# An encoder trunk on eight cores: the 31-tap depthwise convolution as a four-phase block convolution instead of diagonal matmuls

## Chip, cores and metric

The kernel runs on one Trainium2 chip, on all 8 cores, each with its own quarter of one sequence (two dies of four cores). The metric is the device time of the slowest core in microseconds. Some executions fall into a slower state: the cores of one die (of both in one of the runs) show a lower granted TensorE clock, 0.81 to 0.97 instead of 0.98, and the program takes 1 to 17% longer. In the fast runs all eight cores show 0.96 to 0.99, mostly 0.98.

In some runs that still count as fast, two cores of one die sit at a clock of 0.96 to 0.97 and finish 10 to 20 us late. Where that happened it is said, and "clean" means a fast run in which no core did so. "Slow clock": behind a wait the profile shows a granted clock of 0.50, in before for 3.4 to 10.5 us and once, at the gap between the halves, for 34 us. Eight matmuls then take up to 3.57 us instead of 1.89 (before, at 1028.45 us). The first projection's eight take 3.57 us too, but there the record still shows 1.00.

## The reference, cut to what matters

Two layers; every layer is a token mixer, a cross-attention into 256 memory tokens and a SwiGLU block, each behind an RMSNorm and with a residual add. Only the mixer of layer 0 is rebuilt by the change.

```python
D_A = D_B = 512; A_KERNEL = 31; B_KERNEL = 3        # D_MODEL = 1024, SEQ = 8192

def conv_pair_mixer(n, w_in, a_conv_w, a_conv_b, a_ln_g, a_ln_b, b_conv_w, b_conv_b, w_out):
    z = n @ w_in                                        # (B, S, 2560)
    a_val, a_gate, b_h, b_gb, b_gc = jnp.split(z, [...], axis=-1)
    # A: GLU -> depthwise conv (31, centred) -> LayerNorm over channels -> swish
    a = a_val * jax.nn.sigmoid(a_gate)
    a = depthwise_conv(a, a_conv_w, a_conv_b)
    a = jax.nn.silu(layer_norm(a, a_ln_g, a_ln_b))
    # B: B * conv3(C * h)
    b = b_gb * depthwise_conv(b_gc * b_h, b_conv_w, b_conv_b)
    return jnp.concatenate([a, b], axis=-1) @ w_out
```

## The kernel before

Each core has 2048 tokens and works through them in two halves of 1024; a half is two tiles of 512 tokens. Channels lie on the partitions, tokens along the free dimension. The program is a list of operations per engine; a "slot" object records who wrote and who read a buffer, and the semaphore waits follow from it. A small queue of deferred operations (`push`, `tick`) drops the RMSNorm squares and scalings between matmul groups. Weights stream through `NS = 4` slots of SBUF, all issued from GpSimd.

The A convolution multiplies each of four blocks of 128 channels by 31 diagonal matrices and accumulates over the taps in PSUM. Of the 128 rows that feed one output row of such a matmul only one carries anything but zeros. The order of the mixer is: A projection, A convolution with its LayerNorm, B projection, B convolution with its gate, output projection.

```python
    def setup_diag(self, js, with_b, after=()):          # built by GpSimd at the start
        for j in js:
            for k0 in range(0, 31, 4):
                ...
                P.op("pool", "tensor_tensor", [self.ident_s, self.vec_s] + list(after), [self.diagA_s[j]],
                     out=self.diagA[:, j, k0:k0 + nk, :], in0=<identity>, in1=<taps>, op=ALU.mult)
        ...                                              # diagB likewise, 3 taps

    def l0_mixer(self):
        tiles = [(tt, TT) for tt in range(NTT)] + [(-1, H2)]     # two tiles of 512, then the halo of 2x16 tokens
        ...
        for tt, n in tiles:
            for j in range(4):
                bv = self.linear(...)                    # value and gate projections
                bg = self.linear(...)
                ...                                      # a_ext[:, j, ...] = value * sigmoid(gate)
        self.flush(keep="setup")
        for tt in range(NTT):
            for j in range(4):
                b = self.bank()
                pairs = [(self.diagA[:, j, k, :], self.a_ext[:, j, tt * TT + k + 1:tt * TT + k + 1 + TT])
                         for k in range(31)]
                self.mm_group(b, pairs, TT, reads=[self.a_ext_s[j], self.diagA_s[j]])
                cb.append(b)
            ...                                          # ac = conv + bias; acb = ac; sqa = ac**2
            self.mm_group(b1, [(self.ones[:, :], self.acb[:, j, :]) for j in range(4)], TT, ...)   # sums over
            self.mm_group(b2, [(self.ones[:, :], self.sqa[:, j, :]) for j in range(4)], TT, ...)   # the channels
            ...                                          # mean, rstd; y[:, j] = silu((ac - mean) * rstd * g + b)
        ...                                              # B: project h and C, multiply into a_ext
        for tt in range(NTT):
            for j in range(4):
                pairs = [(self.diagB[:, j, k, :], self.a_ext[:, j, tt * TT + k:tt * TT + k + TT]) for k in range(3)]
                self.mm_group(bcv, pairs, TT, reads=[self.a_ext_s[j], self.diagB_s])
                bgb = self.linear(...)
                ...                                      # y[:, 4 + j] = (conv + bias) * gate
        self.proj_residual("ev_out", 0, self.y, self.y_s, KC, nxt=V_GXA)
```

Between the halves the final norm goes through a separate buffer `nf`, is stored, and then x of the next half is loaded and normalised:

```python
            for tt in range(NTT):
                self.store_tile(h, tt, jobs[tt])
                if h + 1 < NHALF:
                    self.load_tile(h + 1, tt)
                    if tt == 0:
                        self.load_halo(h + 1)
```

The softmax here doesn't subtract the row's maximum and nothing guards it: scores larger than these inputs give would overflow.

## Time and profile before

| | us |
|---|---|
| median of 16 runs | 1992.5 |
| fast runs | 1990.7 to 1995.7 |
| the two slow runs among them | 2325.8, 2335.3 |

The first fence is from the page of the profile. The numbered lines give busy time (share of the span) and instructions of each engine; a line of the groups reads: source line, engine, operation, output<-inputs, shape, count | busy us, mean ns | idle time of the engine just before.

```profile
span 1989.4 us, 24567 instructions; the slowest of 8 cores (1970.3 to 1989.4 us)
...
PE 1845.9 (93%) x8826; PEld 839.5 (42%) x8826; DVE 619.6 (31%) x968; ACT 576.7 (29%) x961; POOL 118.1 (6%) x194
...
PE 84%; DVE 4%; ACT 4%; DMA 4%; issue 3%; DVEq 0%; SPq 0%; ACTq 0%; POOLq 0%
...
L401 PE MATMUL ps<-a_ext,diagA 128*128 128x512 bf16 x496 | 109.9, 383 | 0.0
```

TensorE (PE) is busy 93% of the span, and the chain of work that ended last (the third line shown) is 84% TensorE. So time is to be had only from fewer matmul columns or from TensorE's 143.5 us of idle time. The diagonal convolution is 496 matmuls of 512 columns and 109.9 us.

The list of what TensorE waited for; the columns are total us, times, and the longest wait:

```profile
PE ps L72 <- ACT sq L72: 54.0, 22, 13.1
PE ps L401 <- DVE nT L72: 27.3, 4, 12.8
...
PE ps L401 <- DMA wbuf<-w_xq: 10.4, 4, 3.5
PE ps L401 <- DVE a_ext L72: 8.3, 2, 7.7
```

The timeline of TensorE, from several windows; the columns are start, duration (us), engine, line, operation, output<-inputs, shape, count, and in brackets the idle time before it with what released it:

```profile
38.60 3.57 PE L401 MATMUL ps<-nT,wbuf 128*128 128x512 bf16 x8 [12.79 <-DVE nT L72]
...
83.82 1.02 PE L401 MATMUL ps<-nTh,wbuf 128*128 128x32 bf16 x32 [7.67 <-DVE a_ext L72]
84.67 28.97 PE L401 MATMUL ps<-a_ext,diagA 128*128 128x512 bf16 x124
...
117.10 26.98 PE L401 MATMUL ps<-a_ext,diagA 128*128 128x512 bf16 x124
...
148.75 14.69 PE L401 MATMUL ps<-nT,wbuf 128*128 128x512 bf16 x64
...
197.69 5.34 PE L401 MATMUL ps<-y,wbuf 128*128 128x512 bf16 x24
...
231.29 1.04 PE L401 MATMUL ps<-memnT,wbuf 128*128 128x256 bf16 x8
...
1028.45 3.57 PE L401 MATMUL ps<-nT,wbuf 128*128 128x512 bf16 x8 [7.20 <-DVE nT L72]
```

These lines are milestones. The first projection starts at 38.6 us. The A convolution with its sums runs from 84.7 to 148.75 us. The output projection begins at 197.69, and at 231.29 the keys of the memory tokens follow. The second half's first projection starts at 1028.45 us, 31.7 us after the first half's last matmul of the down projection.

VectorE (same columns): at the start the eight scalings of x tile 0, 1.36 us each, and later one product.

```profile
27.55 10.90 DVE L72 SCALAR_TENSOR_TENSOR nT<-hT,vec,rs 128x512 bf16<-128x512 f32 x8 [27.55 <-ACT rs L72]
...
157.94 0.69 DVE L72 TENSOR_TENSOR ac<-ac,rs 128x512 f32<-128x512 f32 x1
```

### The profile page before, as it was taken

Reading aid. Unit: us, or ns where it says so; the run is one execution under the profiler, and the core shown is the slowest. Engines: PE = TensorE matmul, PEld = TensorE weight load, DVE = VectorE, ACT = ScalarE, POOL = GpSimd, SP = SyncE. Lnnn points to the kernel's source line nnn. Section 1 sums busy time; section 2 is a strip of 40 time slices with the busy share of each in tenths; the row PEclk is TensorE's granted clock in tenths of the full one; section 3 lists DMA queues with packets and bytes.
Section 4 is the critical chain, followed back from the end, with each engine's and each line's share of the span. In section 5 each row is a group of like instructions: output and inputs, shape, how many; then the busy total and the mean of one; then the engine's idle time right before and its main releaser. Section 6 shows DMA issues by size and latency. Waiting matters only on the chain.

```text
span 1989.4 us, 24567 instructions; the slowest of 8 cores (1970.3 to 1989.4 us)
## 1 busy us (share of the span) xinstructions
PE 1845.9 (93%) x8826; PEld 839.5 (42%) x8826; DVE 619.6 (31%) x968; ACT 576.7 (29%) x961; POOL 118.1 (6%) x194
## 2 busy tenths in 40 slices
PE   3899899999989899999949999999999999999996
PEld 0344444444434444444414444444444444444443
DVE  2423415121156324121132423342111661532113
ACT  2323353111133353111142423531111433521111
POOL 8000000000000000000000000000000000000000
PEclk9899999999999999999969999999999999999998
DMA  7204662433434632334352067233345327234252
GB/s 169 43 1 74 99 104 43 74 68 69 81 59 86 112 58 49 79 64 88 61 182 44 1 106 127 43 54 74 64 88 93 64 51 143 41 64 85 51 88 85
DMA packets 28949, 150.60 MB, mean 76 GB/s; under 512 B 2976, under 2 KB 3360, under 8 KB 17440
## 3 DMA queue, kind: packets, MB, share of 16 engines
q0 software_dynamic: 21456, 130.30, 37.0%
q1 hardware_dynamic: 7376, 18.74, 3.0%
q8 instruction: 74, 1.21, 0.2%
q14 instruction: 43, 0.35, 0.1%
HBM read 270.92 MB, written 8.39 MB: 140 GB/s over the span
## 4 chain that ended last, share of the span: by engine, by line
PE 84%; DVE 4%; ACT 4%; DMA 4%; issue 3%; DVEq 0%; SPq 0%; ACTq 0%; POOLq 0%
PE ps L401 82%; DMA wbuf<-w_xq 2%; PE ps L72 2%; DVE nT L72 2%; DMA hT<-x_in 2%; ACT t L72 1%; ACT L72 1%; DVE nf L72 1%; ACT pT L72 1%; ACT sq L72 1%; ACT rs L72 1%; DVE hT L72 0%; PE ps L723 0%; DVE v_ln L72 0%; DVE memnT L72 0%
## 5 line engine op out<-in xcount | busy, mean ns | idle before, releaser
L401 PE MATMUL ps<-nT,wbuf 128*128 128x512 bf16 x4224 | 935.9, 382 | 30.4 <-DVE nT L72 20.0
L401 PEld LDWEIGHTS ps<-nT,wbuf 128*128 128x128 bf16 x4224 | 413.5, 98 | 528.4 <-issue 48.2
L72 ACT ACTIVATE t<-ps 128x512 f32<-128x512 f32 (+1 forms) x288 | 164.2, 574 | 566.2 <-PE ps L401 539.1
L401 PE MATMUL ps<-hid,wbuf 128*128 128x512 bf16 x1408 | 313.7, 379 | 0.0
L72 ACT ACTIVATE sq<-hT 128x512 bf16<-128x512 f32 x224 | 137.9, 627 | 484.5 <-DVE hT L72 439.4
L72 DVE TENSOR_TENSOR hid<-ps,t 128x512 bf16<-128x512 f32 x176 | 121.0, 691 | 468.9 <-PE ps L401 468.9
L72 DVE TENSOR_TENSOR hT<-hT,ps 128x512 f32<-128x512 f32 x192 | 130.8, 687 | 384.1 <-PE ps L401 384.1
L401 PEld LDWEIGHTS ps<-hid,wbuf 128*128 128x128 bf16 x1408 | 137.7, 98 | 165.8
L72 DVE SCALAR_TENSOR_TENSOR nT<-hT,vec,rs 128x512 bf16<-128x512 f32 x192 | 135.7, 774 | 90.6 <-ACT rs L72 90.6
L72 PE MATMUL ps<-sq,ones 128*128 128x512 bf16 (+2 forms) x248 | 89.6, 386 | 54.4 <-ACT sq L72 54.0
L401 PE MATMUL ps<-y,wbuf 128*128 128x512 bf16 x512 | 123.3, 391 | 8.8 <-ACT t L72 8.8
L401 PE MATMUL ps<-oT,wbuf 128*128 128x512 bf16 x512 | 118.3, 379 | 8.5 <-DVE oT L72 4.8
L401 PE MATMUL ps<-a_ext,diagA 128*128 128x512 bf16 x496 | 109.9, 383 | 0.0
L72 DVE TENSOR_TENSOR oT<-ps,rs 128x512 bf16<-128x512 f32 x64 | 41.1, 686 | 192.1 <-PE ps L401 164.2
L401 PEld LDWEIGHTS ps<-y,wbuf 128*128 128x128 bf16 x512 | 51.0, 100 | 73.7 <-issue 17.2
L401 PEld LDWEIGHTS ps<-oT,wbuf 128*128 128x128 bf16 x512 | 49.4, 98 | 70.2 <-issue 12.2
L72 ACT ACT_TABLE_LOAD x43 | 55.2, 1283 | 64.7 <-PE ps L72 22.8
L401 PEld LDWEIGHTS ps<-a_ext,diagA 128*128 128x128 bf16 x496 | 48.5, 98 | 60.2 <-issue 2.7
L401 PE MATMUL ps<-wbuf,nT 128*128 128x512 bf16 x256 | 58.9, 393 | 7.4 <-DVE nT L72 7.4
L72 PEld LDWEIGHTS ps<-sq,ones 128*128 128x128 bf16 x248 | 24.4, 100 | 93.7 <-issue 70.6
L72 ACT ACTIVATE qT<-ps 128x512 bf16<-128x512 f32 x64 | 38.2, 597 | 87.3 <-PE ps L401 87.3
L75 POOL DMA_DIRECT2D wbuf<-w_fg x24 | 12.7, 530 | 651.6 <-PE ps L401 651.6
(76 smaller groups left out, 801.0 us busy)
## 6 DMA issues: line engine op xcount, KB each, us to landing
wbuf<-w_fd POOLq DMA_DIRECT2D x32, 704.0 KB, 6.6
wbuf<-w_fg POOLq DMA_DIRECT2D x20, 1024.0 KB, 8.3
wbuf<-w_fu POOLq DMA_DIRECT2D x20, 1024.0 KB, 11.5
wbuf<-w_ev_in POOLq DMA_DIRECT2D x20, 512.0 KB, 8.3
hT<-x_in SPq DMA_DIRECT2D x16, 512.0 KB, 14.4
wbuf<-w_xk POOLq DMA_DIRECT2D x8, 1024.0 KB, 8.7
wbuf<-w_xv POOLq DMA_DIRECT2D x8, 1024.0 KB, 10.0
wbuf<-w_xq POOLq DMA_DIRECT2D x8, 1024.0 KB, 13.3
```

Of the source, the lines that this page charges most:

```text
L72: return self.add(eng, lambda e: getattr(e, meth)(**kw), reads, writes)
L75: return self.add(eng, lambda e: e.dma_start(**kw), reads, writes, dma=sem)
L401: ins = e.matmul(ps[:, 0:n], lhsT=l, rhs=r, start=(i == 0), stop=(i == np_ - 1))
```

## The change

The intent is to use all 128 rows of TensorE for useful work. Tokens are split by their position modulo 4 (four phases). A block then has 32 channels times 4 input phases on the rows and the same 32 channels times 4 output phases in the columns, so that 31 taps become 9 block taps over 256 columns: 144 matmuls of 256 columns a half instead of 248 of 512. The price is data movement: the GLU result has to be regrouped from "128 channels, one phase after the other" to "32 channels x 4 phases" by SBUF-to-SBUF transfers ("relayout"), the result has to be regrouped back, and the block matrices are not kept in SBUF: four slabs of 1.18 MB (as bf16) are loaded for each half.

Other parts of the change: the 3-tap B convolution moves to ScalarE and VectorE; the order of the mixer becomes A projection, first half of the B projection, A convolution, rest of B, output projection; the halo is projected second; memory setup comes later; the diagonals go; there are five weight slots; and the next half's x is staged in `xs` and normalised under the last down projection.

```diff
-NS = 4
-WSLOT = 4096
+NS = 5
+WSLOT = 4608
 ...
+    def ld_conv(self, g, after=()):
+        ...
+        self.P.dma("pool", f"w{i}", list(after), [self.wbuf_s[i]], out=flat, in_=self.conv_w[g])
 ...
-        tiles = [(tt, TT) for tt in range(NTT)] + [(-1, H2)]
+        order = [(0, TT), (-1, H2), (1, TT)]
 ...
+        for i in range(PH):
+            for s in range(PH):
+                P.dma_part(("sp", "act")[i % 2], f"rl{i}", self.X_s[i], s == 0, self.a_ph_s,
+                           out=self.X[CG * s:CG * (s + 1), i, :, :], in_=self.a_ph[CG * i:CG * (i + 1), :, s, :])
 ...
+        hc = [self.ld("ev_in", 0, 1024), self.ld("ev_in", 0, 2048)]
+        cv += [self.ld_conv(1, self.X_s), self.ld_conv(2, self.X_s)]
 ...
+        stage_b(0, *hc, order)                            # first half of the B projection
+        for i in range(PH):
+            wv, ws = cv[i]
+            for q in range(2):
+                    for jj in range(2):
+                        for m in range(NTAP):
+                            ins = e.matmul(self.ps[b][:, jj * NPH:(jj + 1) * NPH], lhsT=wv[:, 2 * q + jj, m, :],
+                                           rhs=self.X[:, i, 2 * q + jj, m:m + NPH], ...)
+            ...                                           # evict to cst
+            if i == 0:
+                cv.append(self.ld_conv(3))
+            conv_b(i // 2, i % 2)
+            for r in range(PH):
+                P.dma_part("sp", "rb", self.acT_s[0], (i, r) == (0, 0), self.cst_s[i],
+                           out=self.acT[CG * i:CG * (i + 1), :, r, :], in_=self.cst[CG * r:CG * (r + 1), i, :, :])
 ...
+        stage_b(1, *hc, order[:2])
+        stats(0)                                          # acb, sqa from acT
+        stage_b(1, *hc, order[2:])
+        s0 = sums(0)
+        h0 = head(0, *s0)                                 # mean, rstd
+        conv_b(2, 0)
+        conv_b(3, 0)
+        stats(1)
+        gate_b(0)
+        tail(0, *h0)                                      # y[:, 0:4] of tile 0
+        conv_b(2, 1)
+        conv_b(3, 1)
+        gate_b(1)
+        s1 = sums(1)
+        tail(1, *head(1, *s1))                            # y[:, 0:4] of tile 1
         self.proj_residual("ev_out", 0, self.y, self.y_s, KC, nxt=V_GXA)
 ...
+                    if more:
+                        for tt in range(NTT):
+                            self.load_tile(h + 1, tt, staged=True)
+                        self.load_halo(h + 1)
+                    jobs = self.ffn(1, more)              # first_norms(True) goes in front of the down projection
```

## The prediction

> Times are for the fast state (before: 1990 us; two of its four runs were slow).
>
> **What bounds it.** TensorE: the page gives PE 1845.9 of 1989.4 us busy (93%), VectorE 31%, ScalarE 29%; the chain of waits is 84% PE. Only fewer matmul columns or shorter PE gaps (143 us) pay. From PE timeline, stage table and list of waits:
> - start: first projection at 38.6 us; x tile 0 lands by 24 us, and its eight scalings take 10.9 us (1.36 us each, 0.75 later) while GpSimd builds diagonals;
> - A convolution with its LayerNorm sums: 83.8 to 148.75 us, 65 us a half, 248 matmuls of 512 columns and 3.7 us of waits;
> - B convolution: 8 x 0.65 us a half;
> - a 7.7 us wait at the halo in half 1;
> - between halves: 997 to 1028.4 us, PE busy 4.9 of 31.4 us;
> - four waits for query weights, 10.4 us.
>
> **What the change does.**
> 1. A convolution in four phases: 32 channels x 4 phases on the partitions, 9 block taps for 31: 144 matmuls of 256 columns a half. On the memory tokens such matmuls come 0.11 us apart, so weight loads (98 ns) stay hidden.[...] 16 us + 3.6 us of sums replace 65 us: -90 us in both halves.
> 2. B convolution to ScalarE and VectorE, under 40% busy: -10 us.
> 3. Halo second, memory setup later: -8 us.
> 4. Tile 0 first, no diagonals: first projection at about 25 us, -13 us.
> 5. Next half's x staged and normalised under the last down projection, final norm in place: -27 of the 31 us gap.
> 6. A fifth weight slot: query waits -8 us.
> 7. Added: 16 relayout transfers each way a half, and four conv-weight slabs of 1.18 MB (as bf16) a half. Where DMA is saturated (share 1.00), weights come at 152 to 175 GB/s: about 7 us a slab (estimate), for 4 us of matmuls. Slabs 2 and 3 are requested once the relayout has landed, slab 4 after the first conv group, the next projection's weights behind. The first B projection (14 us) covers the relayout[...], no more. I expect PE waits of 12 us in half 1 and 18 us in half 2, where 8.4 MB of stores and reloads of x share the SP queue with half the relayouts: +30 us.
>
> PE is the limit, so nearly all counts: -156 + 30[...]: about -132 us.
>
> **Predicted: 1857 us, 8 in 10 between 1828 and 1888.** Faster by over 2%: 0.96; within 2%: 0.03; slower: 0.01.
>
> **What would show it.** PE busy near 1745 us; 288 conv matmuls 0.11 us apart; first projection near 25 us; no PE gap between halves; new PE waits on conv slabs, the relayout or the projection behind, about 30 us; DMA share near 1.00 there; query waits near 0; other stages unchanged.
>
> **What would make it wrong.** Slower relayout transfers (runs of 528 bytes and 1 KB; no trace here has such); convolution matmuls bound by weight loads after all; x reloads delaying the relayout in half 2; ScalarE or VectorE holding PSUM banks while waiting for the relayout back; or, for the better, conv slabs fully hidden (about 1830 us).[...]

The author's -132 us are -156 + 30 = -126 and about 6 us more for a slow clock, an estimate for which the text gives no reading; without the term the sum is -126 us. The 152 to 175 GB/s are the author's reading of before; in steps of 10 us it shows 140 to 197 GB/s where the DMA share is 0.97 or more, outside the start and the gap (250 to 260 us: 175, 690 to 700 us: 156).

## The result, and the profile after

| | before | after |
|---|---|---|
| median, us | 1992.5 (16 runs) | 1909.3 (10 runs) |
| fast runs, us | 1990.7 to 1995.7 | 1905.6 to 1909.7 |
| ratio of fast runs | | 0.9579, interval 0.9570 to 0.9588 |

Ratios are the mean time of one kernel's fast runs over that of the other's in the same rounds, so they are not quite the ratio of the medians quoted. The change gains 83 us by the medians, 4.2%, where the prediction had 132 us, with a range of 1828 to 1888 us. The direction was right. The time lies 21 us above the upper end of the range.

The page of the profile after, and below it the list of TensorE's waits:

```profile
span 1907.8 us, 24146 instructions; the slowest of 8 cores (1891.7 to 1907.8 us)
...
PE 1763.4 (92%) x8570; PEld 816.8 (43%) x8570; DVE 633.8 (33%) x992; ACT 581.3 (30%) x965; POOL 83.6 (4%) x164
...
PE 79%; DVE 7%; ACT 6%; issue 4%; DMA 4%; ACTq 0%; SPq 0%; DVEq 0%; POOLq 0%
...
L656 PE MATMUL ps<-X,wbuf 128*128 128x256 bf16 x288 | 36.0, 288 | 16.2 <-DMA wbuf<-conv_w 14.7
```

```profile
PE ps L78 <- ACT sq L78: 32.9, 15, 11.6
PE ps L656 <- DMA wbuf<-conv_w: 14.7, 4, 5.1
PE ps L417 <- DVE nT L78: 14.6, 3, 7.3
...
PE ps L417 <- DVE a_ph L78: 8.3, 5, 3.9
PE ps L417 <- ACT acb L78: 8.2, 2, 4.2
PE ps L417 <- ACT y L78: 8.0, 3, 3.5
PE ps L417 <- DMA wbuf<-w_ev_in: 6.2, 2, 3.9
...
PE ps L417 <- DVE hT L78: 3.9, 1, 3.9
```

The convolution itself did what it should: 109.9 us became 36.0 us, and TensorE's busy time fell by 82.5 us (1845.9 to 1763.4). But TensorE's idle time, span less busy, is 144.4 us after 143.5 us before. In the list of waits 44 us of old ones went (squares 54.0 to 32.9, scalings 27.3 to 14.6, query weights 10.4 to 0), and 35 us came under new names: conv slabs 14.7, `y` 8.0 and 1.0 more on VectorE, input weights 6.2, `hT` 3.9, `b_ext` 1.5. The halo's wait changed its name from `a_ext` to `a_ph` and kept its 8.3 us. The idle time that the list does not explain grew by the rest.

The timeline of TensorE after, for the same milestones:

```profile
31.21 3.57 PE L417 MATMUL ps<-nT,wbuf 128*128 128x512 bf16 x8 [7.28 <-DVE nT L78]
...
57.24 0.57 PE L417 MATMUL ps<-nTh,wbuf 128*128 128x32 bf16 x16 [3.87 <-DVE a_ph L78]
60.26 19.42 PE L417 MATMUL ps<-nT,wbuf 128*128 128x512 bf16 x80 [2.44 <-DVE a_ph L78]
84.35 0.47 PE L78 MATMUL ps<-sq,ones 128*128 128x256 bf16 x2 [4.67 <-ACT sq L78]
...
118.67 5.77 PE L656 MATMUL ps<-X,wbuf 128*128 128x256 bf16 x36 [5.10 <-DMA wbuf<-conv_w]
...
164.30 3.61 PE L417 MATMUL ps<-y,wbuf 128*128 128x512 bf16 x16 [2.13 <-ACT y L78]
...
183.30 3.12 PE L417 MATMUL ps<-y,wbuf 128*128 128x512 bf16 x8 [3.85 <-DVE hT L78]
...
202.89 2.78 PE L417 MATMUL ps<-memnT,wbuf 128*128 128x256 bf16 x24 [2.21 <-ACT t L78]
...
964.40 1.89 PE L417 MATMUL ps<-nT,wbuf 128*128 128x512 bf16 x8
```

Cutting both spans at the same milestones gives a ledger. Layer 0 runs from the first projection to the first key matmul of the memory tokens; the gap runs from the last down-projection matmul of the first half to the first projection of the second, whose line at 964.40 us above has no bracket and so no wait.

| stretch, us | before | after | change | predicted |
|---|---|---|---|---|
| start to first projection | 38.6 | 31.2 | -7.4 | -13 |
| layer 0, half 1 | 192.7 | 171.7 | -21.0 | -46 |
| rest of half 1 | 765.5 | 761.5 | -4.0 | -4 |
| gap between the halves | 31.7 | 0.0 | -31.7 | -27 |
| layer 0, half 2 | 183.0 | 163.9 | -19.1 | -32 |
| rest of half 2 and end | 777.9 | 779.5 | +1.6 | -4 |
| span | 1989.4 | 1907.8 | -81.6 | -126, and -6 for the clock term |

The predicted column deals out the items of the prediction: in half 1, -45 and -5 for the convolutions, -8 for halo and setup, +12 for waits; in half 2, -45, -5 and +18; the 8 us of query waits half and half. Almost all that is missing lies in the two layer-0 stretches, 38 us, and 6 us each at the start and in the last row.

Two more readings after. VectorE at the start: the same eight scalings take half as long, and start hardly earlier (25.67 against 27.55 us).

```profile
25.67 5.39 DVE L78 SCALAR_TENSOR_TENSOR nT<-hT,vec,rs 128x512 bf16<-128x512 f32 x8 [25.67 <-ACT sq L78]
```

The transfers, in the list of DMA issues (queue, count, KB of one, median us from issue to landing):

```profile
wbuf<-conv_w POOLq DMA_DIRECT2D x8, 1152.0 KB, 14.9
...
acT<-cst SPq DMA_DIRECT2D x32, 128.0 KB, 16.8
...
X<-a_ph SPq DMA_DIRECT2D x16, 66.0 KB, 4.4
X<-a_ph ACTq DMA_DIRECT2D x16, 66.0 KB, 5.4
```

A conv slab takes 14.9 us from issue to landing where the prediction's estimate was 7 us, and a returning piece of 128 KB takes 16.8 us. The return runs beside weight loads that are asked for at the same moment (in half 1 the last slab at 106.2 us, the first returning piece at 106.6, B weights at 106.7), and experiment 1, which leaves three of the four slabs out, brings it down to 7.5 us.

### The profile page after: what moved, and what is told of

Its sections match the earlier page's. It is cut to its first block, busy times and chain, and to the rows that moved or that the text cites. A ratio compares the mean times of both kernels' runs of the same rounds, so it can differ in the third digit from the quotient of the medians.

```text
span 1907.8 us, 24146 instructions; the slowest of 8 cores (1891.7 to 1907.8 us)
## 1 busy us (share of the span) xinstructions
PE 1763.4 (92%) x8570; PEld 816.8 (43%) x8570; DVE 633.8 (33%) x992; ACT 581.3 (30%) x965; POOL 83.6 (4%) x164
## 3 DMA queue, kind: packets, MB, share of 16 engines
q0 software_dynamic: 22608, 139.73, 42.3%
q8 instruction: 72, 1.18, 0.2%
## 4 chain that ended last, share of the span: by engine, by line
PE 79%; DVE 7%; ACT 6%; issue 4%; DMA 4%; ACTq 0%; SPq 0%; DVEq 0%; POOLq 0%
PE ps L417 75%; PE ps L78 3%; DVE nT L78 2%; DMA wbuf<-conv_w 2%; ACT t L78 2%; DVE hT L78 1%; DVE t L78 1%; ACT L78 1%; DMA hT<-x_in 1%; PE ps L656 1%; ACT pT L78 1%; DMA wbuf<-w_ev_in 1%; ACT rs L78 1%; DMA acT<-cst 0%; DVE a_ph L78 0%
## 5 line engine op out<-in xcount | busy, mean ns | idle before, releaser
L78 ACT ACTIVATE t<-ps 128x512 f32<-128x512 f32 (+1 forms) x288 | 164.0, 574 | 587.6 <-PE ps L417 559.0
L78 ACT ACTIVATE sq<-hT 128x512 bf16<-128x512 f32 x208 | 126.7, 626 | 384.3 <-DVE hT L78 354.2
L78 DVE SCALAR_TENSOR_TENSOR nT<-hT,vec,rs 128x512 bf16<-128x512 f32 x176 | 119.2, 746 | 79.6 <-ACT rs L78 54.0
L78 PE MATMUL ps<-sq,ones 128*128 128x512 bf16 (+2 forms) x248 | 84.9, 373 | 33.8 <-ACT sq L78 32.9
L656 PE MATMUL ps<-X,wbuf 128*128 128x256 bf16 x288 | 36.0, 288 | 16.2 <-DMA wbuf<-conv_w 14.7
L78 ACT ACTIVATE rs<-t 128x512 f32<-128x512 f32 x67 | 41.2, 615 | 8.1 <-ACT t L78 0.4
L417 PEld LDWEIGHTS ps<-wbuf,nT 128*128 128x128 bf16 x256 | 25.6, 101 | 40.1 <-issue 11.9
## 6 DMA issues: line engine op xcount, KB each, us to landing
wbuf<-w_ev_in POOLq DMA_DIRECT2D x20, 512.0 KB, 14.6
wbuf<-conv_w POOLq DMA_DIRECT2D x8, 1152.0 KB, 14.9
```

What stands on the lines that cost most here:

```text
L78: return self.add(eng, lambda e: getattr(e, meth)(**kw), reads, writes)
L417: ins = e.matmul(ps[:, 0:n], lhsT=l, rhs=r, start=(i == 0), stop=(i == np_ - 1))
L656: ins = e.matmul(self.ps[b][:, jj * NPH:(jj + 1) * NPH], lhsT=wv[:, 2 * q + jj, m, :], rhs=self.X[:, i, 2 * q + jj, m:m + NPH], start=(m = ...
```

## The experiments

All kernels are edits of the kernel after, except where stated. "Against after" is worked out from the two ratios to before (after: 0.9579) or, where named, from clean runs.

The first theory was that the missing gain had gone into the transfers: slabs and relayouts later than thought. Its rivals were the engines behind the new order (LayerNorm directly before the output projection), and ScalarE being held up by issuing transfers.

### 1. One conv slab for all groups (wrong result)

```diff
-        cv += [self.ld_conv(1, self.X_s), self.ld_conv(2, self.X_s)]
+        cv += [cv[0], cv[0]]
+        self.ws_i += 2
...
-                cv.append(self.ld_conv(3))
+                cv.append(cv[0])
+                self.ws_i += 1
```

> After with all four convolution groups reading weight slab 0, slabs 1 to 3 never loaded (wrong result on purpose): 3.5 of 4.7 MB less weight traffic a half. After has TensorE waiting 14.7 us for conv weights and 6.2 us for the projection weights behind them. Theory W (late weights ate the missing gain, some 50 us against the prediction): 30 us or more faster than after, about 1875. Theory O (the missing gain lies in the strict order of ScalarE and VectorE, and in a convolution term counted too large): only those waits[...] go, 16 to 24 us, about 1888, and the waits on ScalarE and VectorE in layer 0 stay.

Measured: 1880.0, 1881.2, 1890.5, 1891.8 us (the last two with two cores at a clock of 0.97), ratio 0.9466 [0.9433, 0.9498]: 22 us below after, 28 us in clean runs. The slab waits went from 14.7 to 0, and with them the waits on `acb` (8.2) and `hT` (3.9). The waits on `y` rose from 8.0 to 13.0. So six slab loads cost more than the wait named after them: the returning pieces of 128 KB, which took 16.8 us (median) in after, land in 7.5 us here, so the slab loads also delay the way back.

### 2. No relayout (wrong result)

The matmuls read `a_ph` directly and the statistics read `cst` directly. Slabs 2 and 3 now wait for `a_ph` instead of `X` and so are requested earlier, and the output projection's weights no longer wait for the way back (not shown in the cut).

```diff
-        for i in range(PH):
-            for s in range(PH):
-                P.dma_part(("sp", "act")[i % 2], f"rl{i}", self.X_s[i], s == 0, self.a_ph_s, ...)
...
-        cv += [self.ld_conv(1, self.X_s), self.ld_conv(2, self.X_s)]
+        cv += [self.ld_conv(1, self.a_ph_s), self.ld_conv(2, self.a_ph_s)]
...
-                                           rhs=self.X[:, i, 2 * q + jj, m:m + NPH], start=(m == 0),
+                                           rhs=self.a_ph[:, 2 * q + jj, i, m:m + NPH], start=(m == 0),
...
-            for r in range(PH):
-                P.dma_part("sp", "rb", self.acT_s[0], (i, r) == (0, 0), self.cst_s[i], ...)
```

> After without any relayout transfer, either way: the convolution reads the un-relaid buffer and the LayerNorm reads the convolution's own output (wrong result on purpose; same matmuls, same ScalarE and VectorE work). Theory R (the relayout's latency is what is exposed): the 8.2 us of waits at the LayerNorm sums, the 5 to 7 us of transfer issue on ScalarE a half, and earlier slabs 2 and 3: 20 us or more faster, about 1885. Theory W: under 8 us faster, since slabs still cost 7 us each. Theory O: about 12 us faster, the part that ScalarE's issue of transfers and its late statistics cost.

(The 7 us a slab are the prediction's estimate from before's 152 to 175 GB/s; in after a slab takes 14.9 us from issue to landing.)

Measured: 1881.8 to 1884.7 us in three fast runs (one slow run of 1971.9), ratio 0.9452 [0.9432, 0.9473]: 25 us below after. Waits on `acb` gone, slab waits down to 6.3, waits on `y` up to 12.8 and on input weights from 6.2 to 8.0.

### 3. Neither slabs 2 to 4 nor relayouts (wrong result)

Both edits above in one kernel. The first slab and the projection weights are still loaded.

> Slab 0 for all groups and no relayout, together (wrong result on purpose). Alone these gave about 22 and 25 us against after. Theory D (one crowd: slabs, projection weights and relayout wait for the same transfer engines, so each is late because of the other): the two overlap, 30 to 36 us together, about 1873. If they were separate costs they would add: 47 us, about 1861. Whatever is left above the predicted 1857 plus 30 (that is, 1827 with no cost of transfers in layer 0) is then not transfers: theory O expects 1865 to 1880, 40 us or more left.

Measured: 1871.9 and 1873.9 us, and two slow runs; ratio 0.9407 [0.9384, 0.9430], 35 us below after. The single effects add up to 47, so they overlap: each alone takes part of the same wait away. In the ledger layer 0 loses 18.1 us in half 1 (171.7 to 153.6) and 17.1 us in half 2. The prediction had 12 and 18. **The transfers taken out cost what was predicted, within 5 us, and cannot be the bulk of the shortfall.** Without them layer 0 is 39.1 and 36.2 us shorter than before, where the prediction without its +30 says 58 and 50. So 33 us are still missing. About 7 of these are transfers too: in half 2 TensorE waits 2.51 and 4.16 us for weights of the B projection (`w_ev_in`), a wait that before did not have, while SyncE stores and reloads x and the DMA share stands at 0.94 to 1.06 (950 to 980 us).

TensorE's timeline of this kernel around the output projection of half 1, and the second of these two waits:

```profile
139.85 1.03 PE L417 MATMUL ps<-sqa,ones 128*128 128x512 bf16 x4
143.37 15.66 PE L417 MATMUL ps<-y,wbuf 128*128 128x512 bf16 x64 [2.49 <-ACT y L78]
162.28 3.57 PE L417 MATMUL ps<-y,wbuf 128*128 128x512 bf16 x8 [3.25 <-ACT y L78]
...
183.05 2.78 PE L417 MATMUL ps<-memnT,wbuf 128*128 128x256 bf16 x24 [2.21 <-ACT t L78]
...
987.57 6.88 PE L417 MATMUL ps<-nT,wbuf 128*128 128x512 bf16 x24 [4.16 <-DMA wbuf<-w_ev_in]
```

From the end of the sums (140.9 us) to the memory keys is 42.2 us, where before it was 33.6 for the same 128 matmuls (half 2: 42.3 against 34.6). The stretch here holds 8 of the next norm's sums of squares and before's held 14, at 0.22 us each, so like for like the difference is about 1.3 us a half more. TensorE waits for `y` twice, and the first eight matmuls after the second wait take 3.57 us instead of 1.89. This pointed to the LayerNorm.

### 4. Output projection reads only the B half of y (wrong result)

```diff
-                b = self.linear(slab, ss, ml, kc, lambda k, sl=sl: src[:, k, sl],
+                b = self.linear(slab, ss, ml, kc, lambda k, sl=sl: src[:, 4 + k % 4 if name == "ev_out" else k, sl],
...
-        self.proj_residual("ev_out", 0, self.y, self.y_s, KC, nxt=V_GXA)
+        self.proj_residual("ev_out", 0, self.y, self.y_s[4:] + self.y_s[4:], KC, nxt=V_GXA)
```

> After with the output projection of layer 0 reading the B half of its input twice, so that TensorE never waits there for the LayerNorm's output (wrong result on purpose; same matmuls). VectorE and ScalarE still do the LayerNorm tail ahead of the residual adds. Without any transfers in layer 0 the projection stage was still 8 us a half longer than before (42.2 and 42.3 us against 33.6 and 34.6). Theory L (the LayerNorm, which before finished long ahead of the output projection, now ends right in front of it): TensorE's 8 us of waits on the LayerNorm's output go, part comes back as waits for PSUM behind VectorE: 6 to 12 us faster, about 1899. If L is wrong: within 2 us.

Measured: 1902.1 to 1903.7 us, ratio 0.9556 [0.9541, 0.9571]: 5 us. The waits on ScalarE's `y` went from 8.0 to 0, but 7.4 us of waits on VectorE's half of `y` and 2.9 on `hT` appeared: VectorE still does the LayerNorm in front of what TensorE now asks for. Not waiting for the result is not the same as not doing the work.

### 5. No LayerNorm after the sums (wrong result)

On top of experiment 3: the projection reads only the B half of `y`, and reciprocal root, subtraction, product and Silu are not done at all.

```diff
-            rstd = self.rstd_bc(b2, TT, 1.0 / 512, LN_EPS, extra_sub=msq)
-            return mean, rstd
+            P.op("dve", "tensor_scalar", [self.ps_s[b2]], [msq.slot], out=msq.t[:, 0:16], ...)
+            return mean, msq
...
-            for j in range(4):
+            for j in ():
```

> The run without slabs and relayout, and also without the LayerNorm's tail: sums and means are kept, the 1/sqrt, the eight scalings and the swish of each tile are not done, and the output projection reads the B half twice (wrong result on purpose; same matmuls). Theory L: the 16 us that the output projections were longer than in before go, 12 to 18 us faster than the run without transfers, about 1858. If the LayerNorm is covered: within 3 us of it, about 1872, and the missing time of layer 0 stays unexplained.

Measured: 1851.1 to 1851.7 us in four fast runs, ratio 0.928 [0.9263, 0.9296], 21.5 us below experiment 3. Layer 0 is 142.0 and 135.4 us: 11.6 and 11.4 us less. The expectation was 12 to 18; it was more. TensorE's timeline shows the same stretch without a wait until the last norm, and 30.5 us long:

```profile
141.97 15.70 PE L417 MATMUL ps<-y,wbuf 128*128 128x512 bf16 x72
...
172.42 2.78 PE L417 MATMUL ps<-memnT,wbuf 128*128 128x256 bf16 x24 [0.93 <-ACT t L78]
```

Against before's output projection (33.6 and 34.6 us) the LayerNorm's place costs 8.6 + 7.7 = 16 us with most transfers out of the way (about 19 with the same number of sums of squares); taking it out altogether gives 23.

### 6. LayerNorm of tile 1 earlier

```diff
+        conv_b(2, 1)
+        conv_b(3, 1)
         stats(1)
         gate_b(0)
         tail(0, *h0)
-        conv_b(2, 1)
-        conv_b(3, 1)
-        gate_b(1)
-        s1 = sums(1)
-        tail(1, *head(1, *s1))
+        gate_b(1, (0, 1))
+        h1 = head(1, *sums(1))
+        gate_b(1, (2, 3))
+        tail(1, *h1)
```

> After with the second tile's LayerNorm sums in the middle of its gate projection, and the B convolutions all ahead, so that VectorE is through the LayerNorm tail when the residual adds of the output projection begin. Theory O: the waits at the output projection (3.9 us on residual adds, 8.0 us on the LayerNorm output) mostly go with their slow clock: 8 to 14 us faster, about 1897. Theories W and R: within 2 us of after.

Measured: 1905.1, 1919.0, 1924.6, 1926.0 us, ratio 0.963 [0.958, 0.968]. Inconclusive: three of the four runs had two or four cores at 0.964 to 0.970. The one clean run and the undisturbed die of the profile (median 1899.3 us, 1903.2 in after) say at most 3 to 4 us. The waits moved to `acb` (10.8) and `cst` (6.1), so this shift alone is not enough.

### 7. All relayout transfers of half 1 issued from SyncE

ScalarE's timeline after shows why this was tried:

```profile
78.36 5.22 ACTq L85 DMA_DIRECT2D X<-a_ph  x8
83.68 0.72 ACT L78 ACTIVATE sq<-mst 128x256 bf16<-128x256 f32 x2 [6.65 <-issue]
```

Issuing eight transfers held ScalarE for 5.22 us, and TensorE waited 4.67 us for the square behind them (the line at 84.35 us above); the eight matmuls next to it, at the slow clock, took 3.45 us instead of 1.89. The issue costs ScalarE 0.65 us for each transfer of 66 KB, where the transfers land 5.4 us (median) after issue; in half 2 the eight held ScalarE for 6.87 us.

```diff
-                P.dma_part(("sp", "act")[i % 2], f"rl{i}", ...
+                P.dma_part(("sp", "sp" if first else "act")[i % 2], f"rl{i}", ...
```

> After with the eight relayout transfers that ScalarE issues moved to SyncE in the first half (second half unchanged). In after ScalarE spends 5.2 us issuing them while TensorE waits 4.7 us for its squares and then runs 1.6 us at the slow clock. Theory O: about 6 us faster, about 1902, and the 4.7 us wait gone. Theories W and R: 0 to 1 us, or slower, as the relayout now leaves from one queue and slabs 2 and 3 follow later.

Measured: 1902.2 to 1907.8 us in three fast runs, ratio 0.9561 [0.9543, 0.9578]: about 3 us. The wait on squares fell from 32.9 to 27.3, but the waits on `y` rose to 15.7. The time was given back further on, at the LayerNorm.

### 8. Reload of x tile 1 after the relayout and the way back

In half 2 SyncE is busy with the residual reload of x until 1005.9 us before it can issue its half of the relayout.

```diff
+        if not first:
+            self.load_tile(1, 1)
...
-                if more:
+                if more and tt == 0:
```

> After with the reload of x tile 1 (second half) issued by SyncE behind the relayout instead of ahead of it. In after SyncE is stuck in that reload until 1005.9 us, the relayout lands at 1017 us though its input was ready at 999.5, and TensorE then waits 9.6 us for slabs 2 to 4. Theory D, second half (the prediction's queue conflict): relayout and slabs some 7 to 10 us earlier, 5 to 9 us faster, about 1901. If the slabs' own rate is the limit: within 2 us.

Measured: 1898.8, 1902.6, 1919.7 us (the last with cores at 0.962) and two slow runs; ratio 0.9596 [0.9537, 0.9655], which says nothing. Layer 0 of half 2 went from 163.9 to 157.0 us in the profile, and the clean runs are about 8 us below after. So the delay in half 2 is probably real, some 7 us of the 17 that the transfers cost there; two clean runs and one profile are all that says so.

### 9. GpSimd multiplies at the start, twice

The prediction's start had two parts: x tile 0 alone first, and no diagonals. These kernels put multiplies of the diagonals' size back on GpSimd, into a scratch buffer: 18 of them in the first, 28 in the second.

```diff
+            for i in range(28):
+                P.op("pool", "tensor_tensor", [self.ones_s, self.vec_s], [self.dscr_s], ...)
```

> After with 18 of the diagonal multiplies put back on GpSimd at the start (into a scratch tile nobody reads; result stays correct). If the start was won by the diagonals' removal, since VectorE's first eight scalings took 1.36 us each beside them and 0.75 us without, the first projection moves from 31.2 to about 36 us and the whole by +5, about 1913. If it was won by the new order of the loads: no change.

Measured with 18: 1905.3 to 1910.1 us, ratio 0.958 [0.9562, 0.9598], no change. It told little: the multiplies had ended at 24.9 us, when the scalings had just begun (23.9 us; the eight took 6.1 us).

> As the run with 18 multiplies on GpSimd, but 28, so that they last beyond the scalings (the 18 had ended at 24.9 us, before the scalings began, so that run told nothing). If GpSimd's multiplies slow VectorE's scalings, the eight take about 10.9 us as in before instead of 5.4, and the first projection starts at about 36 us instead of 31; the weights behind it are requested later too, so the total may be more than 5 us up. If not, 31 us.

Measured with 28: 1911.1 and 1913.1 us, ratio 0.9601 [0.9580, 0.9622]. The scalings took 11.54 us instead of 5.39, and the first projection started at 35.7 us:

```profile
24.03 11.54 DVE L78 SCALAR_TENSOR_TENSOR nT<-hT,vec,rs 128x512 bf16<-128x512 f32 x8 [24.03 <-ACT sq L78]
```

So some 5 us of the 7.4 us at the start come from the diagonals, and about 2 us from the order of the loads. VectorE is slower while GpSimd multiplies: 0.67 us a scaling without, 1.36 (before) and 1.44 (here) with. What slows it, these runs don't show.

### 10. Halo last, as before

```diff
-        for tt, n in order:
+        for tt, n in (order[0], order[2], order[1]):
```

> After with the halo projected last in the gated unit again, as in before. In after TensorE waits 8.3 us around the halo, VectorE being busy with scaling tile 1. The prediction's step 3 says that halo second saves several us: 3 to 8 slower than after, about 1913. The trace of after says the wait is for tile 1's scaling, which comes whatever stands in front: within 3 us.

Measured: 1908.0, 1910.1, 1911.0 us clean, 1920.5 with cores at 0.964, one slow; ratio 0.9607 [0.9579, 0.9636]. The waits on the GLU result `a_ph` fell from 8.3 to 2.0, but the waits on `nT` rose from 14.6 to 22.3. The halo second moves a wait of 8 us from one name to another and saves 1 to 2 us by the clean runs.

### 11. Next half's norms after the down projection

```diff
+        jobs = self.proj_residual("fd", l, self.hid, self.hid_s, FC, nxt=V_GFIN, final=True)
         if more:
             self.first_norms(True)
             self.tick_n = 4
-        return self.proj_residual("fd", l, self.hid, self.hid_s, FC, nxt=V_GFIN, final=True)
+            self.want(("n", 1))
+        return jobs
```

The line with `want` has the queue run tile 1's norm to its end before layer 0 begins.

> After with the second half's first norms after the down projection instead of under it (x still staged early, so no wait for loads; both tiles and the halo at the boundary). The overlap theory says the gap comes back as the norm chain alone, without the load: 24 squares on ScalarE (about 11 us), two rstd steps, 16 scalings (12 us): +20 to +28 us, about 1932. If the gap was mainly the load of x: under +10.

Measured: 1920.6 to 1921.3 us in three fast runs, ratio 0.9648 [0.9625, 0.9671], 13 us slower than after; the gap is 16.2 us. So about half of the gap's 31.7 us went because the squares and scalings run under the down projection, and half because x is already there (the staging).

### 12. Last store from the staging buffer

The final norm in place writes 2 KB runs of `hT`; this kernel writes it to `xs`, with 4 KB runs as before.

```diff
-        if final:
+        if final == 2:
+            dst = (gcol, lambda k: self.xs[tt][:, k, :], self.xs_s[tt])
+        elif final:
```

> After with the second half's final norm written into the free staging tile, from which a store takes 4 KB runs, instead of in place, from where it takes 2 KB runs. In before the last stores landed in 3.4 us, in after in 7.6 us (medians), and after ends 4.9 us later behind its last residual add. If the run length is the reason: 3 to 4 us faster, about 1904. If it is chance or the order of the last norms: within 1 us.

Measured: 1905.7 to 1907.3 us, ratio 0.9575 [0.9560, 0.9590], within noise of after. The last row of the ledger went from 779.5 to 776.4 us, so the end of the kernel is 3 us shorter in the profile, as far as one profile shows it. The kernel's last eight stores (512 KB each, no loads beside them) land in 3.2 us (median) with 4 KB runs, against 5.7 us with 2 KB runs in after.

### 13. Four weight slots (an unwanted wrong result)

```diff
-NS = 5
+NS = 4
```

> After with four weight slots. If the fifth slot is what removed the four waits for query weights (10.4 us in the profile of before, 3 to 12 on its cores), they come back, 4 to 10 us; and slab 0 and the projection weights of layer 0 are requested later, so more waits there: 10 to 25 us slower than after, about 1925. If the fifth slot does nothing: within 3 us.

Measured: 1939.6 to 1944.3 us, ratio 0.9756 [0.9740, 0.9773]. The result is wrong (relative error 0.42), not on purpose: with four slots the first conv slab takes the slot of value weights that are still to be read. The first projection waits for it until 51.4 us. Half 2 waits the same way, for 16.0 us. Waits on query weights came back to only 5.4 us. The run says no more than that this schedule needs the fifth slot; that the fifth slot removed the query waits stays not shown.

### 14. The measures together

Three variants, all correct. Common to them: relayouts issued from SyncE and GpSimd instead of ScalarE; the first part of the second B projection between conv groups 3 and 4, to cover the last slab and the return; the reload of x tile 1 late; separate statistics buffers for the two tiles, so that the gate projections cover the LayerNorm; the last store from `xs`.

```diff
+                P.dma_part(("sp", "pool")[i % 2], f"rl{i}", ...)     # from the second variant on behind the B weights
...
+        conv(0)
+        conv(1)
+        conv(2)
+        stage_b(1, *hc, order[:2])
+        conv(3)
...
+        for j, tt in ((2, 0), (3, 0), (2, 1), (3, 1)):
+            conv_b(j, tt)
+        stats(0)
+        gate_b(0)
+        gate_b(1, (0, 1))
         s0 = sums(0)
+        stats(1, (0, 1))
         h0 = head(0, *s0)
+        stats(1, (2, 3))
+        gate_b(1, (2, 3))
         s1 = sums(1)
+        tail(0, *h0)
         tail(1, *head(1, *s1))
```

> A version meant to beat after, correct: relayout issued from SyncE and GpSimd instead of SyncE and ScalarE; reload of x tile 1 behind the relayout; weights of the second B projection requested ahead of slab 4, and its first tile run between convolution groups 3 and 4, so that slab 4 and the way back are covered; gate projections ahead of the LayerNorm sums; sums of both tiles in separate buffers; the last stores from the contiguous tile. Theory D + L (schedule, not work): waits in layer 0 fall from some 60 us to 35, 15 to 28 us faster, about 1886. If waits only move: 1900 or more.

Measured for the first variant (relayout on GpSimd ahead of the B weights): 1898.0 to 1905.4 us, ratio 0.9549 [0.9528, 0.9569]. The B projection's weights queued on GpSimd behind the relayout, which waits for data: 31.5 us of waits on `w_ev_in`. That mistake ate most of the gain: 6 us by the ratio, where 15 to 28 were expected.

> The sched version with its fault mended: the first B projection's weights are requested ahead of the relayout again. Sched waited 31.5 us for them, of which after has 6. Theory D + L: waits of TensorE fall by 25 to 30 us and with them the slow clock behind them; 1868 to 1878, 30 to 40 us faster than after, all of it schedule, since the same work is done. If layer 0 is limited by the transfers' total rate, the waits move to the slabs: 1888 or more.

Measured for the second (relayout behind the B weights): 1879.2, 1881.5, 1890.0 us (the last with cores at 0.97), one slow; ratio 0.9463 [0.9433, 0.9492]. Correct, and 23 us below after by the ratio, about 28 in clean runs, short of the 30 to 40 expected. Layer 0 is 160.8 and 149.3 us. The list of TensorE's waits:

```profile
PE ps L669 <- DMA wbuf<-conv_w: 9.6, 3, 4.1
...
PE ps L419 <- ACT X L78: 8.1, 2, 4.7
PE ps L419 <- DVE t L78: 6.8, 2, 4.3
...
PE ps L419 <- DMA wbuf<-w_ev_in: 1.8, 3, 1.0
```

The waits on `acb`, `y` and `hT` (20.1 us in after) are gone, replaced by `X` (now also the second statistics buffer) and `t`, 14.9 us together; the slab waits fell by 5.1 us and those for input weights by 4.4. This kernel beats both.

> sched2 with the first tile's LayerNorm sums ahead of the first half of the second gate projection. It starts the chain to the output projection about 3.5 us sooner, but TensorE may wait for ScalarE's squares there: within 3 us of sched2.

Measured for the third (first gate pair after the head): 1884.5 and 1885.2 us fast, three slow runs, no interval. No gain over the second.

## Why the prediction was wrong in size and right in direction

| item of the prediction | predicted | measured | shown by |
|---|---|---|---|
| 1. A convolution in four phases | -90 | about -85 | experiment 3: 17.4 + 3.6 us for 64.1 us in half 1, 15.8 + 3.6 for 61.7 in half 2 |
| 2. B convolution off TensorE | -10 | about -10 | 16 groups of 0.65 us gone; a wait of 1.5 us on `b_ext` is counted in item 1, and its place ahead of tile 1's LayerNorm (below) in the LayerNorm |
| 3. halo second, setup later | -8 | about 0 | 7.67 us of wait became 3.87 + 2.44 and smaller; experiment 10 |
| 4. start | -13 | -7.4 | ledger; experiment 9 |
| 5. gap | -27 | -31.7, less about 5 for 24 squares moved | ledger; experiment 11 |
| 6. fifth slot, query waits | -8 | -10.4 | list of waits; that the slot did it is not shown |
| 7. transfers | +30 | +35 taken out, about 7 left in | experiment 3 |
| not in it: LayerNorm in front of the output projection | 0 | +16 (stretch) to +23 (removed) | experiments 3 and 5 |
| not in it: end of the kernel | 0 | about +5 | 21.7 us after the last down projection, 16.8 before |

The terms are not disjoint (experiments 1 to 3 show overlap). Added up as they stand, their differences from the prediction make 49 to 56 us, where 49 are missing, so some are counted twice or a little too large; the 6 us of the clock term have no experiment of their own.

**The step that failed is item 7 with the sum behind it ("PE is the limit, so nearly all counts").** The prediction put the new waits of layer 0 at +30 and looked for them in the transfers only. The transfers cost that and somewhat more, 35 us and about 7. Beside them stood the LayerNorm, 16 to 23 us with a predicted cost of 0. Before, 49 us of B projection and B gate lay between the LayerNorm's sums and the output projection, and its reciprocal root, its products and its Silu were free. The new order uses most of this cover for the relayout and the slabs. In after TensorE ends the last sums at 162.2 us while ScalarE's Silu of tile 0 ends at 164.0, and tile 1's LayerNorm has only tile 0's output projection to run under. It also starts late: VectorE takes up tile 1's sums only at 170.49 us, because tile 1's B convolution and gate products (164.85 to 170.5 us) stand ahead of it, and these had first waited 2.57 us for ScalarE. So the work that item 2 moved off TensorE lies on the same way. VectorE's timeline after shows how that ends:

```profile
180.56 0.69 DVE L78 TENSOR_TENSOR t<-t,rs 128x512 f32<-128x512 f32 x1
181.18 4.87 DVE L78 TENSOR_TENSOR hT<-hT,ps 128x512 f32<-128x512 f32 x8
```

The first line is the last product of tile 1's LayerNorm, begun at 170.49 us. Only behind it, in VectorE's order, come the residual adds of tile 0, eight at once: all eight PSUM banks of the output projection had filled up meanwhile. TensorE, finished with eight groups, waits 3.85 us until 183.30 us and then takes 3.12 us for eight matmuls. The list puts this wait down to the residual adds (`hT`), but the bank that TensorE needs next was emptied by the first of them, at 181.9 us; its next group also reads tile 1's `y`, and ScalarE's last Silu for it ended at 183.05. In half 2 and in experiment 3 the list names the wait at this place `y`. In before the same work ran from 147.4 to 158.6 us, most of it under the B projection. A cost model of each engine's load (VectorE 33%, ScalarE 30% busy) cannot see this; the order in one engine's program can. In the prediction's list of what could make it wrong stands "ScalarE or VectorE holding PSUM banks while waiting for the relayout back"; that is near, but it is the relayout again, not the order.

Second, item 3: the halo and the setup were counted as removed while they were moved. The wait set by how fast VectorE makes the GLU result (8.3 us in before and in after) stayed when the order changed. Third, the start was oversized by 5.6 us: tile 0 was to land much earlier, and landed about 2 us earlier, 22 instead of 24 us; only the scalings got faster. Fourth, "PE busy near 1745 us" missed by 18: the matmuls taken away are 109.9 - 36.0 us of the A convolution and 10.4 us of the B convolution, 84 us together, not 101.

What was right: the mechanism of the convolution in full. 36 matmuls of 256 columns take 4.11 us, 0.11 us apart, as on the memory tokens in before (48 in 5.40 us), and the weight loads, one for each matmul and 103 ns long, stayed hidden. (With 512 columns the matmuls come 0.218 us apart, 124 in 26.98 us in before, with a weight load for each as well.) The gap went, the query waits went, and other stages did not change.

What remains open: how the 16 to 23 us of the LayerNorm divide between waits for `y`, waits for PSUM banks and slow matmuls after them, since every run that removed one of them moved it to another; how much of it is the B convolution's place ahead of tile 1's LayerNorm, which no run changed by itself; and why two cores of a die sit at a clock of 0.96 to 0.97 in some runs. Whether the memory setup, whose squares (2.75 us on ScalarE) moved into the first B projection, costs anything there was not tried by itself; the wait of 4.67 us at 84.35 is for the first of them.

## What to carry to other kernels

When a stage gets shorter, ask what it had been covering, and what stands next to the consumer now: here the A convolution lost 85 us, and some 40 us of transfers and about 20 us of LayerNorm that had been free came into view. Cost a changed order engine by engine up to the next consumer, not only the transfers that it adds. And to find where a gain went, take away one suspect and both: the singles here (22 and 25 us) add up to more than the pair (35 us), and only the pair left a remainder of 33 us to look into.
